# Third layer of a four-layer hybrid: the sums of squares of the heads' outputs as two products of operands in two parts

## The chip, the cores and the metric

The kernel runs on one core of one Trainium2 chip. The metric is the device time of one execution in microseconds (us), as the median of the runs taken. Five engines work beside each other, each through its own queue in order: TensorE (PE in the profile, its weight loads PEld), VectorE (DVE), ScalarE (ACT), GpSimd (POOL) and SyncE (SP), which here issues the DMAs.

## The reference

A stack of four residual layers over 1040 tokens (16 learned ones in front of 1024) of width 1024: a sliding-window attention, an mLSTM, an HGRN2 and again an attention. The change is in the third layer. Cut to what matters:

```python
def hgrn2_branch(u, w_in, lower_bound, o_gain, w_out, valid):
    q, fpre, inp, z = _split(u @ w_in, C_SIZES)
    ...
    o = hgrn2_chunkwise(heads(silu(q)), heads(kk), heads(inp), heads(lf))   # 8 heads of width 128
    o = rmsnorm(o, o_gain.reshape(C_HEADS, C_DV)).reshape(bsz, lp, C_W)     # over the 128 of each head
    return (o * silu(z)) @ w_out

def rmsnorm(x, g):
    return x * rsqrt(mean(x * x, axis=-1) + EPS) * g
```

For each head and token the mean of the squares of 128 numbers is needed. Everything is in fp32.

## The kernel before

**Layout.** Activations lie with their features on the 128 partitions and the tokens along the row: `x` as eight tiles of 128 x 1040. Tokens are worked on in three chunks, `CHUNKS`, of 400, 384 and 256 columns. A sum over features is thus a sum over partitions, and is made by a matmul with a 128 x 128 tile of ones (`rones`, type fp32r; `ones` is the same tile seen as fp32).

**Products in parts.** A large projection is made of operands in two parts: `split` (L186 to L188) writes a rounded high part (a cast to fp32r on ACT, L187) and the rest, source minus high part (a subtraction on DVE, L188). `proj` (L254), `proj_v` (L295, L299) and `proj_out` (L337) multiply these parts in three fp32r products. Other matmuls take fp32 operands as they are; the sums of squares of this layer are among them. The second layer's sums of squares (L1001) are already two products of a split operand with `rones`.

**One head of the third layer** (`mixer`, in `layer_c`). The tokens go through five regions `REGIONS`: the first block of 16, then four pairs of blocks of 128 (blocks 0; 1, 2; 3, 4; 5, 6; 7, 8). For each region:

- `level`: tiles `X` by additions on DVE (L1152, L1153, L1145), Exp on ACT (L1154, L1146) and a multiplication on DVE (L1155);
- `levels_mm`: a burst of small products of these on PE (L1168, L1178);
- `tail0`: the results are masked (DVE, L1195), summed (DVE, L1204) into `rd`, and GpSimd copies `rd` to the diagonal blocks of `att` (L1206, four copies);
- `tail1`: a transpose on PE (L1228), and its copy to SBUF, `kT` (ACT, L1230);
- `tail2`, block by block: `po` gets `V` times `att` (PE, L1243) and the state times the decayed queries (PE, L1245); then the state is renewed (PE L1250, DVE L1255), on which the next block's L1245 waits.

Three times in a head a chunk of `po` is complete: after block 3, 6 and 8. `o_evac` (L1259) then copies it to the head's row `R["o", h]` (ACT, L1261) and squares it into a temporary tile (ACT, L1263). Later `o_stat` (L1265) sums the squares over the partitions (PE, L1269), makes the reciprocal root from this (`rstd_from`: ACT Ln L353, Exp L354, in place in the tile that held the squares) and multiplies the row by gain and root (DVE, L1271). `o_stat(0)` comes after block 5, `o_stat(1)` after block 8, and `o_stat(2)` after block 0 of the next head; at the end of the last head it comes last. There are 8 heads and 24 such sums.

**What sets the order.** PE's order is written out: `body` weaves the steps of a head (with a cost in ns each, the first number of `S(...)`) with the projections of the next heads, in proportion to the costs (`weave`, L53). The other engines' instructions are put in order when the kernel is built, by a priority list; those under `hi` (all of `mixer`'s) go ahead of others by `PRIO`. Each engine then works its list strictly in order. Temporary tiles `t` share five slots (`TMPS`); PSUM tiles share eight.

Of the kernel before, what the change touches and what calls it, by code (L numbers as in the profile page):

```python
# [10 lines left out]
F32R = mybir.dt.float32r  # L11
# [4 lines left out]
P = 128  # L16
# [22 lines left out]
ROWS, TMPS, RAWS, YS, QS = 9, 5, 2, 3, 6  # L39
# [69 lines left out]
def hybrid_kernel(ctx: ExitStack, tc: tile.TileContext, ins, out, layers=(0, 1, 2, 3)):  # L109
    nc = tc.nc  # L110
    v, s, g, pe, sp = nc.vector, nc.scalar, nc.gpsimd, nc.tensor, nc.sync
# [5 lines left out]
    tpool = ctx.enter_context(tc.tile_pool(name="tpool", bufs=1))  # L117
# [5 lines left out]
    def nm(x):  # L123
        ctr[0] += 1
        return f"{x}{ctr[0]}"
# [10 lines left out]
    def tmp():  # L136
        return tpool.tile([P, 404], F32, tag="t", name=nm("t"), bufs=TMPS)
# [10 lines left out]
    def psa():  # L148
        return psum("pa", 1)
# [4 lines left out]
    rones = cpool.tile([P, P], F32R, name="ones")  # L154
    ones = rones.bitcast(F32)
# [30 lines left out]
    def split(src, h, l):  # L186
        s.copy(h, src)  # L187
        v.tensor_tensor(l, src, h.bitcast(F32), op=ALU.subtract)  # L188
# [163 lines left out]
    def rstd_from(acc, dst, cn, n):  # L352
        s.activation(dst[:, :cn], acc[:, :cn], AF.Ln, bias=eps, scale=1.0 / n)  # L353
        s.activation(dst[:, :cn], dst[:, :cn], AF.Exp, scale=-0.5)  # L354

    def hi(fn):
        def f():
            with tc.high_priority(offset=PRIO):
                fn()

        return f
# [687 lines left out]
    def layer_c(i, j, fin):  # L1049
        win, wout = ins["c_win"][j], ins["c_wout"][j]  # L1050
        R = {}
# [74 lines left out]
        REGIONS = ((0,), (1, 2), (3, 4), (5, 6), (7, 8))  # L1126

        def mixer(h):
            vs = slice((h % 2) * P, (h % 2) * P + P)
            W = {}  # L1130
# [101 lines left out]
            def tail2(r, b):  # L1232
                blkno = REGIONS[r][b]
                c0, cn = blk(blkno)
                n = [blkno in z for z in CHUNK_BLOCKS].index(True)
                if blkno == CHUNK_BLOCKS[n][0]:
                    if n == 0:
                        R["o", h] = row()
                    W["po"] = psum("po", 1)
                oc = slice(c0 - CHUNKS[n][0], c0 - CHUNKS[n][0] + cn)  # L1240
                V = R["v", h // 2, blkno]
                att = W["att", r] if r == 0 else W["att", r][:, b, :]
                pe.matmul(W["po"][:, oc], V[:cn, vs], att, start=True, stop=(r == 0))  # L1243
                if r:
                    pe.matmul(W["po"][:, oc], W["S"], W["qA", r][:, P * b : P * b + P], start=False, stop=True)  # L1245
                if blkno == CHUNK_BLOCKS[n][-1]:
                    o_evac(n)
                if blkno < NB - 1:
                    pc = psa()
                    pe.matmul(pc[:, :P], W["kT", r][:cn, P * b : P * b + P], V[:cn, vs], start=True, stop=True)  # L1250
                    Sn = R["mix"].tile([P, P], F32, tag="S", name=nm("S"), bufs=2)
                    if r == 0:
                        v.tensor_copy(Sn, pc[:, :P])
                    else:
                        v.scalar_tensor_tensor(Sn, W["S"], W["eL", r][:, b : b + 1], pc[:, :P],  # L1255
                                               op0=ALU.mult, op1=ALU.add)
                    W["S"] = Sn

            def o_evac(n):  # L1259
                c0, cn = CHUNKS[n]  # L1260
                s.copy(R["o", h][:, c0 : c0 + cn], W["po"][:, :cn])  # L1261
                W["sq", n] = sq = tmp()
                s.activation(sq[:, :cn], W["po"][:, :cn], AF.Square)  # L1263

            def o_stat(n):  # L1265
                c0, cn = CHUNKS[n]
                o, sq = R["o", h][:, c0 : c0 + cn], W["sq", n]
                st = psa()
                pe.matmul(st[:, :cn], ones, sq[:, :cn], start=True, stop=True)  # L1269
                rstd_from(st, sq, cn, 128)  # L1270
                v.scalar_tensor_tensor(o, o, R["ogain"][:, h : h + 1], sq[:, :cn], op0=ALU.mult, op1=ALU.mult)  # L1271

            def S(cost, fn, *a):
                return [cost, hi(lambda: fn(*a)), None]

            main, tails = [], []
            for r in range(5):
                lvs = list(range(8)) if r else [3, 4, 5, 6, 7]
                st = []
                for lv in lvs:  # L1280
                    st.append(S(0.0, level, r, lv))
                    st.append([GAP, lambda: None, None])
                st.append(S(BURST if r else 0.2 * BURST, levels_mm, r, lvs))
                st.append(S(0.0, tail0, r))
                main.append(st)
                ts = [S(214 if r else 107, tail1, r), [KT_LAG, lambda: None, None]]
                for b in range(len(REGIONS[r])):
                    ts.append(S(640, tail2, r, b))
                    if REGIONS[r][b] in (5, 8):
                        ts.append(S(666, o_stat, 0 if REGIONS[r][b] == 5 else 1))  # L1290
                tails.append(ts)
            return main, tails, S(427, o_stat, 2)

        fg = {h: f_proj(h) for h in range(8)}
        qg = {h: q_proj(h) for h in range(8)}
# [8 lines left out]
        for h in range(8):  # L1304
            fill = qg[0][2] if h == 0 else []
            if h in (4, 6):
                fill += flat(outs(oc[h - 3]))
            if h < 7:
                fill += flat(fg[h + 1]) + flat(qg[h + 1])
            if h in (1, 3, 5):  # L1310
                fill += flat(vg[h // 2 + 1])
            for z in {2: (0, 1), 4: (2,), 5: (3,), 7: (4, 5, 6)}.get(h, ()):
                fill += flat(zg[z])
            main, tails, end = mixer(h)
            if h:
                tails[0].append(held)
            held = end
            mx = []
            for r in range(5):
                mx += weave(main[r], last)  # L1320
                last = [[TAIL_LAG, lambda: None, None]] + tails[r]
            body += weave(mx, fill)
# [8 lines left out]
    for pos, i in enumerate(layers):  # L1331
# [30 lines left out]
        else:  # L1362
            h0, h1 = (sum(z[0] for z in head[k]) for k in range(2))
            seq = flat(head)
            for n, t0, t1, end in ((2, h0 + h1 * FIRST[2], h0 + h1 * FIRST[3], h0 + h1), (1, h0 * FIRST[0], h0 * FIRST[1], h0)):
                st = norm.stats(n, PARTS[n])
# [139 lines left out]
```

## Time and profile before

| | us |
|---|---|
| median of 3 runs | 2607.71 (2605.75 to 2611.24) |
| the profiled execution | 2610.83 |
| its span, first to last instruction | 2609.0 |
| PE busy, of the span | 2558.0 (98%) |
| DVE busy | 1980.3 (76%) |
| ACT busy | 1725.9 (66%) |
| POOL busy | 154.1 (6%) |
| granted TensorE clock, mean | 0.995 |

Busy is the time in which an engine had at least one instruction at work. PE's matmuls overlap each other, so their spacing (from one start to the next), not their recorded length, tells what they take from PE's time. Rows of the timeline give start and length in us, engine, line, operation, tiles written and read, and shape; in brackets the idle time before and what ended it. The third layer's mixers run from about 1590 to 2125 us of the span: the first small `level` tiles on DVE are at 1588.7, the last sum of squares on PE at 2122.1.

### The profile page before, as it was taken

The page shows a single profiled execution, that of the slowest core. Times are in us where ns is not written, and L with a number is a line of the kernel's source. Part 1 is how long each engine was busy: PE and PEld are TensorE (multiplying, and loading weights), DVE is VectorE, ACT ScalarE, POOL GpSimd, SP SyncE. Part 2 cuts the span into 40 slices and gives each one's busy share as a digit, 9 for nine tenths or more (in the row PEclk, how much of TensorE's full clock was granted, in tenths as well). Part 3 has the DMA queues.
Part 4 walks back from the last instruction along what each step waited for, and adds up shares of the span by engine and source line. Part 5 has one row for each costly group of instructions (what it writes and reads, how often), then busy time and mean ns, then how long its engine had stood idle before and what let it go on. Part 6 is the DMA issues. An engine that isn't in the chain of part 4 may idle for free.

```text
span 2609.0 us, 56062 instructions
## 1 busy us (share of the span) xinstructions
PE 2558.0 (98%) x21048; PEld 2459.0 (94%) x21048; DVE 1980.3 (76%) x5487; ACT 1725.9 (66%) x4757; POOL 154.1 (6%) x538
## 2 busy tenths in 40 slices
PE   7999999999999999999999999999999999999999
PEld 6899889899999999999999999999999999999999
DVE  6677777986767676767677788978787978677776
ACT  6777776566464646464646857878585867768872
POOL 1100100000000000000000000201001011000000
PEclk9999999999999999999999999999999999999999
DMA  4111111021111111111110101011110111111112
GB/s 136 56 43 50 46 37 47 17 67 58 41 58 41 58 41 58 41 58 41 55 61 34 57 27 42 30 38 34 34 42 26 42 62 45 54 44 47 53 38 82
DMA packets 74048, 126.81 MB, mean 49 GB/s; under 512 B 11552, under 2 KB 25760, under 8 KB 73776
## 3 DMA queue, kind: packets, MB, share of 16 engines
q1 hardware_dynamic: 73776, 123.23, 14.5%
q8 instruction: 165, 2.70, 0.4%
q14 instruction: 107, 0.88, 0.1%
HBM read 108.34 MB, written 4.26 MB: 43 GB/s over the span
## 4 chain that ended last, share of the span: by engine, by line
PE 81%; DVE 10%; ACT 6%; issue 1%; DMA 1%; POOL 0%; SPq 0%; DVEq 0%; ACTq 0%; POOLq 0%
PE pj L254 39%; PE pj L337 16%; PE pj L299 11%; PE po L682 2%; PE pt L660 1%; PE pm L614 1%; PE pm L615 1%; DVE t L407 1%; PE pa L534 1%; DVE ul L188 1%; PE po L918 1%; PE pj L295 1%; PE pm L890 1%; DVE X L1153 1%; DVE X L1155 1%
## 5 line engine op out<-in xcount | busy, mean ns | idle before, releaser
L254 PE MATMUL pj<-uh,wh 128*128 128x384 f32 (+2 forms) x2592 | 870.9, 336 | 3.7 <-ACT uh L187 3.6
L254 PE MATMUL pj<-ul,wh 128*128 128x384 f32 (+2 forms) x2592 | 835.3, 322 | 2.9 <-DVE ul L188 2.8
L254 PE MATMUL pj<-uh,wl 128*128 128x384 f32 (+2 forms) x2592 | 832.9, 321 | 0.1
L254 PEld LDWEIGHTS pj<-uh,wh 128*128 128x128 f32 x2592 | 491.3, 190 | 24.1 <-issue 12.7
L254 PEld LDWEIGHTS pj<-ul,wh 128*128 128x128 f32 x2592 | 491.2, 190 | 8.7 <-DVE ul L188 5.5
L254 PEld LDWEIGHTS pj<-uh,wl 128*128 128x128 f32 x2592 | 490.9, 189 | 0.5 <-DVE wl L188 0.4
L188 DVE TENSOR_TENSOR wl<-wr,wh 128x512 fp32r<-128x512 f32 x336 | 227.9, 687 | 58.1 <-ACT wh L187 55.4
L340 DVE TENSOR_TENSOR x<-x,pj 128x384 f32<-128x384 f32 (+2 forms) x480 | 235.4, 510 | 43.2 <-PE pj L337 41.3
L187 ACT CAST wh<-wr 128x512 fp32r<-128x512 f32 x337 | 203.3, 616 | 83.0 <-PE pj L337 26.8
L299 PE MATMUL pj<-wh,uh 128*128 128x256 f32 x896 | 258.1, 288 | 0.0
L337 PE MATMUL pj<-yh,wh 128*128 128x384 f32 (+2 forms) x768 | 253.0, 329 | 0.0
L299 PE MATMUL pj<-wh,ul 128*128 128x256 f32 x896 | 252.4, 282 | 0.0
L299 PE MATMUL pj<-wl,uh 128*128 128x256 f32 x896 | 252.3, 282 | 0.0
L337 PE MATMUL pj<-yl,wh 128*128 128x384 f32 (+2 forms) x768 | 247.4, 322 | 3.1 <-DVE yl L188 3.1
L337 PE MATMUL pj<-yh,wl 128*128 128x384 f32 (+2 forms) x768 | 246.8, 321 | 0.0
L299 PEld LDWEIGHTS pj<-wh,uh 128*128 128x128 f32 x896 | 169.3, 189 | 1.1 <-issue 0.3
L187 ACT CAST yh<-r 128x400 fp32r<-128x400 f32 (+2 forms) x144 | 68.6, 477 | 153.2 <-PE pj L337 141.7
L299 PEld LDWEIGHTS pj<-wl,uh 128*128 128x128 f32 x896 | 169.3, 189 | 0.5
L299 PEld LDWEIGHTS pj<-wh,ul 128*128 128x128 f32 x896 | 169.3, 189 | 0.0
L428 ACT ACTIVATE t<-t 128x384 f32<-128x384 f32 (+2 forms) x240 | 117.8, 491 | 76.5 <-DVE t L427 74.8
L427 DVE SCALAR_TENSOR_TENSOR t<-pj,t 128x384 f32<-128x384 f32 (+2 forms) x192 | 98.8, 514 | 78.2 <-ACT t L426 75.3
L337 PEld LDWEIGHTS pj<-yl,wh 128*128 128x128 f32 x768 | 144.9, 189 | 5.0 <-DVE yl L188 4.7
(265 smaller groups left out, 5431.4 us busy)
## 6 DMA issues: line engine op xcount, KB each, us to landing
wr<-in_b_win SPq DMA_DIRECT2D x128, 256.0 KB, 2.6
wr<-in_a_win SPq DMA_DIRECT2D x80, 256.0 KB, 2.7
wr<-in_c_win SPq DMA_DIRECT2D x64, 256.0 KB, 2.7
r<-rowsd SPq DMA_DIRECT2D x16, 520.0 KB, 5.4
wr<-in_a_wout SPq DMA_DIRECT2D x32, 256.0 KB, 2.7
wr<-in_b_wout SPq DMA_DIRECT2D x32, 256.0 KB, 2.6
t<-t SPq DMA_DIRECT2D x96, 48.0 KB, 1.9
wr<-in_c_wout SPq DMA_DIRECT2D x16, 256.0 KB, 2.7
```

The costliest lines, as they stand in the source:

```text
L187: s.copy(h, src)
L188: v.tensor_tensor(l, src, h.bitcast(F32), op=ALU.subtract)
L254: pe.matmul(acc[:, :cn], a[:, k, :], b[:, k, c0 : c0 + cn], start=(k == 0 and i == 0), stop=(k == KT - 1 and i == 2))
L295: pe.matmul(acc[:48, :256], um[:, k, :], m[:, kk, :], start=(k == 0 and m is wh), stop=(k == KT - 1 and m is wl))
L299: pe.matmul(acc[:cn, :256], a[:, k, c0 : c0 + cn], m[:, kk, :], start=(k == 0 and i == 0), stop=(k == KT - 1 and i == 2))
L337: pe.matmul(acc[:, :cn], a[:, k, mc], b, start=(k == 0 and i == 0), stop=(k == 1 and i == 2))
L340: v.tensor_tensor(x[:, m, c0 : c0 + cn], x[:, m, c0 : c0 + cn], acc[:, :cn], op=ALU.add)
L407: v.scalar_tensor_tensor(u, x[:, k, cs], ngain[:, self.i, k : k + 1], self.acc[n], op0=ALU.mult, op1=ALU.mult)
L427: v.scalar_tensor_tensor(a[:, :cn], z, 0.0, a[:, :cn], op0=ALU.min, op1=ALU.subtract)
L428: s.activation(a[:, :cn], a[:, :cn], AF.Exp)
L534: pe.matmul(st[:, 2 * k : 2 * k + 2], sq[:, z : z + P], R["masks"][:, 0:P:64], start=True, stop=True)
L682: pe.matmul(po[64 * hh : 64 * hh + 64, q0 - c0 : q0 - c0 + nq], V[kb][:kn, vc : vc + 64], ws[hh]["Pt"][:kn, u, ki, :nq], start=(ki == 0), ...
```

## The change

In `o_evac` the squares are now split at once: the high part goes into a tile `oh` (ACT cast, L187), of which there is one slot, and the rest into a tile `ol` (DVE subtraction, L188), which takes a slot of the `t` tiles until the sum is made. In `o_stat` the one fp32 product with `ones` becomes two fp32r products with `rones` that add up in the same PSUM tile, and a fresh temporary tile takes the root. The costs that the weave uses for the three steps are halved.

```diff
             def o_evac(n):
                 c0, cn = CHUNKS[n]
                 s.copy(R["o", h][:, c0 : c0 + cn], W["po"][:, :cn])
-                W["sq", n] = sq = tmp()
+                sq = tmp()
                 s.activation(sq[:, :cn], W["po"][:, :cn], AF.Square)
+                high = R["mix"].tile([P, 400], F32R, tag="oh", name=nm("oh"), bufs=1)
+                low = tpool.tile([P, 404], F32R, tag="t", name=nm("ol"), bufs=TMPS)
+                W["sq", n] = high, low
+                split(sq[:, :cn], high[:, :cn], low[:, :cn])
 
             def o_stat(n):
                 c0, cn = CHUNKS[n]
-                o, sq = R["o", h][:, c0 : c0 + cn], W["sq", n]
+                o, sq = R["o", h][:, c0 : c0 + cn], tmp()
                 st = psa()
-                pe.matmul(st[:, :cn], ones, sq[:, :cn], start=True, stop=True)
+                for z, part in enumerate(W.pop(("sq", n))):
+                    pe.matmul(st[:, :cn], rones, part[:, :cn], start=(z == 0), stop=(z == 1))
                 rstd_from(st, sq, cn, 128)
...
-                        ts.append(S(666, o_stat, 0 if REGIONS[r][b] == 5 else 1))
+                        ts.append(S(333, o_stat, 0 if REGIONS[r][b] == 5 else 1))
                 tails.append(ts)
-            return main, tails, S(427, o_stat, 2)
+            return main, tails, S(214, o_stat, 2)
```

Each engine's order differs from about the start of the third layer's mixers to their end and is the same again in the fourth layer. Three places, with the program's tile names and numbers (which differ between the two programs for the same tile).

DVE in the first head, where the last pair of blocks is prepared, before the change: the masking L1195 and the sum L1204 of the region with blocks 7 and 8.

```order
L1152 TENSOR_TENSOR X_21759<-r_20881,r_20882 128x64x2
L1271 SCALAR_TENSOR_TENSOR r_20868<-r_20868,ogain_20127,t_21283 128x400
L1195 TENSOR_TENSOR t_21512<-pm_21411,masks_20129 128x192 x2
L1255 SCALAR_TENSOR_TENSOR S_21510<-S_21477,s_21319,pa_21508 128x128
L1204 TENSOR_REDUCE rd_21515<-t_21512 128x64
```

The same place now (L1276 is the line that was L1271):

```order
L1152 TENSOR_TENSOR X_21775<-r_20874,r_20875 128x64x2
L1276 SCALAR_TENSOR_TENSOR r_20893<-r_20893,ogain_20127,t_21489 128x400
L1255 SCALAR_TENSOR_TENSOR S_21520<-S_21481,s_21323,pa_21518 128x128
L1153 TENSOR_TENSOR X_21765<-r_20874 128x16x8
L1153 TENSOR_TENSOR X_21775<-r_20874 128x64x2
L188 TENSOR_TENSOR ol_21515<-t_21512,oh_21514 128x384
L1195 TENSOR_TENSOR t_21522<-pm_21422,masks_20129 128x192 x2
L427 SCALAR_TENSOR_TENSOR t_21502<-pj_21406,t_21502 128x256
L1204 TENSOR_REDUCE rd_21525<-t_21522 128x64
```

The subtraction for the second chunk stands ahead of L1195, so L1195 and all behind it wait for the cast `oh` on ACT. In all eight heads `ol` of the 384 columns stands so, directly or one instruction ahead of this L1195.

ACT at the same place, before: the copy and the Square of the second chunk, among the steps of a projection's sigmoid (L424 to L426).

```order
L354 ACTIVATE t_21283<-t_21283 128x400
L1261 COPY r_20868<-po_21289 128x384
L424 ACTIVATE t_21496<-pj_21460 128x256
L1263 ACTIVATE t_21506<-po_21289 128x384
L425 ACTIVATE t_21496<-t_21496 128x256
L1154 ACTIVATE X_21744<-X_21744 128x256
```

ACT there now:

```order
L354 ACTIVATE t_21489<-t_21489 128x400
L1261 COPY r_20893<-po_21293 128x384
L424 ACTIVATE t_21502<-pj_21406 128x256
L1263 ACTIVATE t_21512<-po_21293 128x384
L425 ACTIVATE t_21502<-t_21502 128x256
L187 CAST oh_21514<-t_21512 128x384
L426 ACTIVATE t_21502<-t_21502,one 128x256
L1154 ACTIVATE X_21770<-X_21770 128x256
```

The cast stands one instruction behind the Square; in the second head an Exp (L354) stands between them.

ACT at the end of the last head, before: copy, Square, a sigmoid's steps, and the roots of the last two sums.

```order
L428 ACTIVATE t_29265<-t_29265 128x400
L1261 COPY r_28572<-po_29301 128x256
L1263 ACTIVATE t_29317<-po_29301 128x256
L424 ACTIVATE t_29325<-pj_29273 128x384
L425 ACTIVATE t_29325<-t_29325 128x384
L426 ACTIVATE t_29325<-t_29325,one 128x384
L353 ACTIVATE t_29203<-pa_29350,eps 128x384
```

And now:

```order
L424 ACTIVATE t_29456<-pj_29409 128x384
L1261 COPY r_28696<-po_29443 128x256
L1263 ACTIVATE t_29477<-po_29443 128x256
L425 ACTIVATE t_29456<-t_29456 128x384
L426 ACTIVATE t_29456<-t_29456,one 128x384
L428 ACTIVATE t_29456<-t_29456 128x384
L187 CAST oh_29479<-t_29477 128x256
L187 CAST wh_29920<-wr_29922 128x512
L353 ACTIVATE t_29502<-pa_29503,eps 128x384
```

The cast of the last chunk stands behind a whole sigmoid, with L428 in it, which waits for DVE's L427. On DVE, `ol` of the last chunk stands behind that sigmoid's L427 and L435. On PE there are now 18 matmuls of 256 columns from the last block's L1245 to the last head's `o_stat(1)`, 6 more to `o_stat(2)`, and behind that the output projection (L337); before, the two sums came after 6 matmuls of 384 and 6 of 256 columns, and after 12 more of 256.

## The prediction

> **What bounds the kernel now.** First the page's busy shares and the chain of work that ended last: is one engine the path, and where not?
>
> ```profile
> PE 2558.0 (98%) x21048; PEld 2459.0 (94%) x21048; DVE 1980.3 (76%) x5487; ACT 1725.9 (66%) x4757; POOL 154.1 (6%) x538
> PE 81%; DVE 10%; ACT 6%; issue 1%; DMA 1%; POOL 0%; SPq 0%; DVEq 0%; ACTq 0%; POOLq 0%
> ```
>
> PE is, but for a sixth of the span the chain runs through DVE and ACT. Next the same for the stretch of the change, in windows (length, then busy time of PE, PEld, DVE, ACT, POOL, the granted clock, DMA). I quote the first, the third, the last but one, and the sum of nine.
>
> ```profile
> 1590.00:1660.00 70.00, 65.38 (x843) 62.72 (x842) 60.70 (x210) 56.37 (x163) 6.56 (x14) 0.98 0.12 39
> ...
> 1720.00:1780.00 60.00, 59.60 (x797) 56.79 (x796) 53.97 (x182) 50.95 (x147) 6.28 (x16) 1.00 0.12 41
> ...
> 2020.00:2080.00 60.00, 58.16 (x792) 55.41 (x791) 55.30 (x187) 50.09 (x143) 6.29 (x16) 1.00 0.12 41
> ...
> sum 540.00, PE 529.81 PEld 507.79 DVE 453.80 ACT 404.47 POOL 56.91; mean PE 58.87 PEld 56.42 DVE 50.42 ACT 44.94 POOL 6.32
> ```
>
> PE idles 10.2 of 540 us, 6.5 of them in the first and the last window quoted, where DVE is at 87% and 92%; in the one between, DVE at 90% cost PE nothing. Over all nine DVE has 86 us to spare. Third, for whom PE waited there (total, times, longest):
>
> ```profile
> PE po L1245 <- DVE S L1255: 5.6, 12, 1.4
> PE pm L1178 <- DVE X L1155: 2.5, 1, 2.5
> ...
> PE po L1243 <- POOL att L1206: 0.6, 1, 0.6
> ```
>
> So the layer is bound by PE, and what it takes off PE counts in full as long as no wait takes its place.
>
> **What the products cost PE.** The 24 sums are 48 records. A 400-column sum, the next matmul but one and the one after it; then a 256-column sum in the same way; then the second layer's sum of 400 columns, which is already two fp32r products.
>
> ```profile
> L1269 PE MATMUL pa<-t,ones 128*128 128x400 f32 (+2 forms) x48 | 18.9, 476 | 0.2 <-ACT v L269 0.2
> ```
>
> ```profile
> 1653.59 0.83 PE L1269 MATMUL pa<-t,ones 128*128 128x400 f32 x2
> ...
> 1654.38 0.28 PE L254 MATMUL pj<-ul,wh 128*128 128x256 f32 x1
> 1654.50 0.28 PE L254 MATMUL pj<-uh,wl 128*128 128x256 f32 x1
> ```
>
> ```profile
> 1741.22 0.59 PE L1269 MATMUL pa<-t,ones 128*128 128x256 f32 x2
> ...
> 1741.83 0.34 PE L254 MATMUL pj<-ul,wh 128*128 128x384 f32 x1
> 1742.00 0.34 PE L254 MATMUL pj<-uh,wl 128*128 128x384 f32 x1
> ```
>
> ```profile
> 902.37 0.34 PE L1001 MATMUL pa<-yh,ones 128*128 128x400 f32 x1
> ...
> 902.74 0.35 PE L254 MATMUL pj<-uh,wh 128*128 128x400 f32 x1
> ```
>
> From 1653.59 to 1654.38 are 0.79 us, with one 256-column matmul in it, which takes 0.12 (1654.38 to 1654.50): the fp32 sum takes 0.67. The pair takes 902.74 - 902.37 = 0.37. Saved: 0.30. For 256 columns: 0.61 less one 384-column matmul of 0.17 is 0.44; the pair would be 2 x 0.12 = 0.24; saved 0.20. For 384 columns by the ratio of columns 0.29. A head saves 0.79, eight heads **6.3 us**.
>
> **What the split adds.** 24 casts and 24 subtractions, priced by those of the output projection, which have the same three shapes:
>
> ```profile
> L187 ACT CAST yh<-r 128x400 fp32r<-128x400 f32 (+2 forms) x144 | 68.6, 477 | 153.2 <-PE pj L337 141.7 <-DVE r L436 9.3 <-DVE x L340 1.1
> L188 DVE TENSOR_TENSOR yl<-r,yh 128x400 fp32r<-128x400 f32 (+2 forms) x144 | 74.0, 515 | 53.5 <-ACT yh L187 53.4
> ```
>
> ACT gets 24 x 0.477 = 11.4 us, DVE 24 x 0.515 = 12.4 us, half a microsecond in three of five regions of a head. DVE's 86 spare us hide that on average. What counts is who stands behind them. `oh` has one slot, so the third cast of a head waits for `o_stat(1)`; in the written order over a hundred matmuls lie between block 8 and `o_stat(2)`, and I cost that at nothing, except at the end of the last head, where it is 24. The steps that the order moves by some matmuls carry no work of their own, and no DMA of this layer changes its place.
>
> **A new wait for `att`.** The order puts `ol` of the second chunk ahead of the masking L1195, which must go through L1204 and four POOL copies before PE's L1243 of block 7. How much room is there? First head: ACT, DVE, POOL, PE.
>
> ```profile
> 1656.73 0.49 ACT L1263 ACTIVATE t<-po 128x384 f32<-128x384 f32 x1
> 1657.10 0.42 ACT L425 ACTIVATE t<-t 128x256 f32<-128x256 f32 x1
> 1657.41 0.42 ACT L1154 ACTIVATE X<-X 128x256 f32<-128x256 f32 x1
> ```
>
> ```profile
> 1656.78 0.62 DVE L1195 TENSOR_TENSOR t<-pm,masks 128x192 f32<-128x192 f32 x2
> 1657.31 0.34 DVE L1255 SCALAR_TENSOR_TENSOR S<-S,s,pa 128x128 f32<-128x128 f32 x1
> 1657.57 0.88 DVE L1204 TENSOR_REDUCE rd<-t 128x64 f32<-128x384 f32 x1
> ```
>
> ```profile
> 1658.57 2.64 POOL L1206 COPY att<-rd 32x64 f32<-32x64 f32 x4 [9.17 <-DVE rd L1204]
> ```
>
> ```profile
> 1661.28 0.47 PE L1243 MATMUL po<-att,v 128*128 128x128 f32 x2
> ```
>
> The copies ended at 1661.21, 0.07 before PE came. Now the chain begins at the Square: Square to the next ACT instruction 0.37, that one 0.31, the cast 0.48, `ol` 0.5, L1195 0.53, one more DVE instruction 0.26, L1204 0.88, to POOL 0.1: 3.4 us, with hops 3.5. With 2.64 for the copies it ends 6.1 us after the Square began, where PE wants it after 1661.28 - 1656.73 = 4.55: PE waits 1.6; with copies of 1.80 (the last head's, below) 0.75. I take 1.2. The second head:
>
> ```profile
> 1719.79 0.50 ACT L1263 ACTIVATE t<-po 128x384 f32<-128x384 f32 x1
> ```
>
> ```profile
> 1721.88 2.23 POOL L1206 COPY att<-rd 32x64 f32<-32x64 f32 x4 [15.04 <-DVE rd L1204]
> ```
>
> ```profile
> 1725.09 0.38 PE L1243 MATMUL po<-att,v 128*128 128x128 f32 x2
> ```
>
> Here the instruction between is an Exp of half a microsecond: 3.7 + 2.23 = 5.9 against 5.30, a wait of 0.6; with 1.80 for the copies 0.2. I take 0.4. In the other six the copies ended well ahead or, in one, already cost the 0.6 of the row above; the last head's:
>
> ```profile
> 2112.80 1.80 POOL L1206 COPY att<-rd 32x64 f32<-32x64 f32 x4 [10.84 <-DVE rd L1204]
> ```
>
> ```profile
> 2116.13 0.38 PE L1243 MATMUL po<-att,v 128*128 128x128 f32 x2
> ```
>
> 1.53 of room; I give the six 0.3 together. Sum **+1.9 us**, bounds 0.5 and 6 (below).
>
> **The end of the last head.** `oh` of the last chunk stands behind a whole sigmoid. The rows before:
>
> ```profile
> 2118.49 0.37 ACT L1261 COPY r<-po 128x256 f32<-128x256 f32 x1 [1.57 <-PE po L1245]
> 2118.76 0.39 ACT L1263 ACTIVATE t<-po 128x256 f32<-128x256 f32 x1
> ...
> 2120.07 0.52 ACT L425 ACTIVATE t<-t 128x384 f32<-128x384 f32 x1
> 2120.62 0.62 ACT L426 ACTIVATE t<-t,one 128x384 f32<-128x384 f32 x1
> ...
> 2122.17 0.51 ACT L428 ACTIVATE t<-t 128x384 f32<-128x384 f32 x1
> ```
>
> From the copy on: copy and Square 0.65, L425 0.5, L426 0.6, DVE's L427, about as long as a subtraction, 0.5, L428 0.5, then DVE's L435 0.5 beside the cast, `ol` 0.45: 3.7, with hops 4.1. PE needs it after 18 x 0.12 + 0.36 + 6 x 0.12 + 0.12 = 3.3. **+0.8**, bounds 0 (if the sigmoid starts earlier) and 1.5. Behind the sum stands an output projection that doesn't need it.
>
> **Sum.** -6.3 + 1.9 + 0.8 = -3.6 us. The profiled execution took 2610.83, its span 2609.0 and 1.8 around it: 2607.2. It lies 3.1 above the median of 2607.71, so against that **2604.1**; with the bounds of the waits (0.5 to 3.0, 0 to 1.5) 2601.9 to 2605.9. The irregular waits at the stretch's start (2.5 for L1155 above) may move either way under the new order; I take 0. A measurement of this kernel can tell about 0.2%, 5.2 us.
>
> **The rivals.**
>
> All hidden: in the new order the casts come soon enough everywhere. For it: the row with 1.53 of room, and only one wait of 0.6 for `att` in the whole layer now. Against it: 0.07 in the first head. 2607.71 - 6.3 = 2601.4, and 1 less if the start's waits shrink as well.
>
> `att` late in every head: POOL's copies get slow.
>
> ```profile
> L1206 POOL COPY att<-rd x128: 226/265/3692, 1626.5 to 2114.4; 32x64 f32<-32x64 f32 x128
> ```
>
> Four at the least would take 0.9 us, yet they took 2.64 in the first head; a copy (least, median and greatest in ns) can take 3.7. With 2.64 everywhere the first two heads wait 1.6 and 1.0; I put the six others between this and nothing, 0.6 each: 6 us. With the 0.8 of the end the gain is gone, -6.3 + 6.8: 2608.2. The Trainium skill, "SBUF — State Buffer", section "Who interferes with whom", has a mechanism for it: a DVE instruction with both inputs in SBUF and a GpSimd instruction that reads SBUF exclude each other, and `ol` has both in SBUF. By that rule 8 subtractions of 0.5 us could hold up the copies by 4 us in all, which would make of the forecast this rival's time. The spread in the row agrees with such a lock; but `ol` stands ahead of L1204, for which the copies wait, so it is over by then, and I add nothing for it.
>
> DVE becomes the path: if its 12.4 us find no cover, every burst L1178 and every L1245 comes later. -6.3 + 12.4 = +6.1: 2613.8, slower. For it: DVE at 92% in a window, and 2.5 + 5.6 us of PE's waits are for DVE. Against it: the window with DVE at 90% and PE at 99%, and 86 us to spare in the sum. It decides from where DVE has no gap left between one burst and the next.
>
> No gain on PE: the pair costs as much as the fp32 sum. The rows at 902 speak against it: 0 + 2.7, 2610.4.
>
> **How the numbers follow.** Forecast 0.52, all hidden 0.25, `att` late everywhere 0.15, DVE the path 0.06, no gain 0.02. Faster by over 0.2%: all hidden and the forecast's lower end, 0.25 + 0.05 = 0.30. Slower: 0.06. The rest, 0.64, within 0.2%. The range reaches from all hidden with a shorter start to `att` late everywhere with a measurement's spread: 2599.8 to 2609.8.
>
> **What would show it.** Right: the 24 sums as pairs, 0.37, 0.36 and 0.24 apart; PE waiting for POOL `att` at L1243 of block 7 in the first two heads, some 2 us in all; a short wait at the last L1274. Wrong: more than 4 us of waits for `att`, or PE's waits for DVE (8.1 us now) grown by over 2; or a gain of more than 6.3, which would have to come from the start of the stretch.

## The result, and the profile after

The changed kernel takes 2613.81 us (median of 22 runs, 2609.18 to 2616.40), the kernel before 2609.24 beside it (22 runs): a ratio of 1.0015, 95% interval 1.0010 to 1.0021. By this ratio it is 3.9 us slower (2.6 to 5.5), where 3.6 us faster was forecast; the two medians lie 4.6 us apart, and all differences below go by ratios. The profiled execution's span is 2612.5 us, 3.5 longer than before.

First the page of the changed kernel, its busy shares and its chain of work:

```profile
PE 2553.9 (98%) x21048; PEld 2456.8 (94%) x21048; DVE 1988.0 (76%) x5511; ACT 1729.0 (66%) x4781; POOL 143.7 (6%) x538
PE 78%; DVE 11%; ACT 7%; DMA 2%; issue 2%; POOL 0%; SPq 0%; DVEq 0%; ACTq 0%; POOLq 0%
```

PE is busy for 4.1 us less, yet the span is longer: PE waits more, and the chain runs more through DVE (11%, it was 10%) and ACT (7%, it was 6%). The same nine windows as before, their sum:

```profile
sum 540.00, PE 522.53 PEld 502.88 DVE 458.53 ACT 407.62 POOL 49.50; mean PE 58.06 PEld 55.88 DVE 50.95 ACT 45.29 POOL 5.50
```

PE idles 17.5 of 540 us now, 10.2 before. For whom it waits (total, times, longest):

```profile
PE po L1245 <- DVE S L1255: 11.6, 13, 2.0
PE po L1243 <- POOL att L1206: 2.5, 3, 1.3
PE pm L1178 <- DVE X L1155: 2.2, 1, 2.2
```

The waits for `att` grew by 1.9 us, the sum that was forecast. The 6.0 us more at L1245, for the renewed state `S`, were in no term of the forecast's sum. The largest of these waits is in head 3 (heads are counted from 0 from here on), between block 1 and block 2. PE before, then PE after, at that place; L1250 gives the product with which DVE renews `S`, the first L1245 behind it reads `S`:

```profile
1815.04 0.39 PE L1250 MATMUL pa<-v,kT 128*128 128x128 f32 x2
1815.18 0.37 PE L299 MATMUL pj<-wh,uh 128*128 128x256 f32 x1
...
1816.68 0.38 PE L1243 MATMUL po<-att,v 128*128 128x128 f32 x2
1817.39 0.49 PE L1245 MATMUL po<-X,S 128*128 128x128 f32 x2 [0.33 <-DVE S L1255]
```

```profile
1812.75 0.39 PE L1250 MATMUL pa<-v,kT 128*128 128x128 f32 x2
1812.98 0.39 PE L1243 MATMUL po<-att,v 128*128 128x128 f32 x2
1815.37 0.49 PE L1245 MATMUL po<-X,S 128*128 128x128 f32 x2 [2.00 <-DVE S L1255]
```

Before, twelve matmuls of a projection (L299) lay between L1250 and L1243; after, none. From L1250 to L1245 it takes 2.35 us before and 2.62 after: DVE's answer hardly changed, but PE has nothing to do meanwhile. What DVE does there now:

```profile
1812.67 0.81 DVE L1204 TENSOR_REDUCE rd<-t 128x64 f32<-128x384 f32 x1
1813.40 0.28 DVE L1152 TENSOR_TENSOR X<-r,r 128x128 f32<-128x128 f32 x1
...
1814.74 0.32 DVE L1155 TENSOR_TENSOR X<-X,Q 128x128 f32<-128x128 f32 x1
1814.98 0.33 DVE L1255 SCALAR_TENSOR_TENSOR S<-S,s,pa 128x128 f32<-128x128 f32 x1
```

DVE works without a gap, in its written order, on `rd`, on `X` tiles and on one tile `v` (L267, in the rows left out), which stand ahead of L1255. There is no `ol` among them.

### The profile page after: what moved, and what is told of

It is laid out like the page before. It is cut to its first block, busy times and chain, and to the rows that moved or that the text cites. A ratio compares the mean times of both kernels' runs of the same rounds, so it can differ in the third digit from the quotient of the medians.

```text
span 2612.5 us, 56091 instructions
## 1 busy us (share of the span) xinstructions
PE 2553.9 (98%) x21048; PEld 2456.8 (94%) x21048; DVE 1988.0 (76%) x5511; ACT 1729.0 (66%) x4781; POOL 143.7 (6%) x538
## 4 chain that ended last, share of the span: by engine, by line
PE 78%; DVE 11%; ACT 7%; DMA 2%; issue 2%; POOL 0%; SPq 0%; DVEq 0%; ACTq 0%; POOLq 0%
PE pj L254 37%; PE pj L337 16%; PE pj L299 11%; PE po L682 2%; PE pt L660 1%; PE pm L614 1%; DVE t L407 1%; PE pm L615 1%; PE pa L534 1%; DVE ul L188 1%; PE po L918 1%; PE pj L295 1%; DVE X L1152 1%; PE pm L890 1%; ACT Sm L639 1%
## 5 line engine op out<-in xcount | busy, mean ns | idle before, releaser
L188 DVE TENSOR_TENSOR wl<-wr,wh 128x512 fp32r<-128x512 f32 x336 | 227.3, 686 | 57.2 <-ACT wh L187 54.3
L187 ACT CAST wh<-wr 128x512 fp32r<-128x512 f32 x337 | 203.3, 617 | 84.1 <-PE pj L337 30.1
L299 PE MATMUL pj<-wh,uh 128*128 128x256 f32 x896 | 257.8, 288 | 0.0
L299 PE MATMUL pj<-wh,ul 128*128 128x256 f32 x896 | 252.7, 282 | 0.0
L299 PE MATMUL pj<-wl,uh 128*128 128x256 f32 x896 | 252.6, 282 | 0.0
L337 PE MATMUL pj<-yh,wh 128*128 128x384 f32 (+2 forms) x768 | 252.3, 329 | 0.0
L337 PE MATMUL pj<-yl,wh 128*128 128x384 f32 (+2 forms) x768 | 247.4, 322 | 3.1 <-DVE yl L188 3.1
L337 PE MATMUL pj<-yh,wl 128*128 128x384 f32 (+2 forms) x768 | 246.9, 321 | 0.0
L428 ACT ACTIVATE t<-t 128x384 f32<-128x384 f32 (+2 forms) x240 | 117.9, 491 | 80.7 <-DVE t L427 79.5
L299 PEld LDWEIGHTS pj<-wh,uh 128*128 128x128 f32 x896 | 169.4, 189 | 0.8 <-issue 0.3
L299 PEld LDWEIGHTS pj<-wl,uh 128*128 128x128 f32 x896 | 169.5, 189 | 0.2
L299 PEld LDWEIGHTS pj<-wh,ul 128*128 128x128 f32 x896 | 169.5, 189 | 0.0
L187 ACT CAST yh<-r 128x400 fp32r<-128x400 f32 (+2 forms) x144 | 68.6, 477 | 151.0 <-PE pj L337 139.5
L427 DVE SCALAR_TENSOR_TENSOR t<-pj,t 128x384 f32<-128x384 f32 (+2 forms) x192 | 98.4, 513 | 74.4 <-ACT t L426 73.2
L337 PEld LDWEIGHTS pj<-yl,wh 128*128 128x128 f32 x768 | 144.9, 189 | 4.7 <-DVE yl L188 4.7
```

The source lines that it names most:

```text
L299: pe.matmul(acc[:cn, :256], a[:, k, c0 : c0 + cn], m[:, kk, :], start=(k == 0 and i == 0), stop=(k == KT - 1 and i == 2))
L337: pe.matmul(acc[:, :cn], a[:, k, mc], b, start=(k == 0 and i == 0), stop=(k == 1 and i == 2))
L427: v.scalar_tensor_tensor(a[:, :cn], z, 0.0, a[:, :cn], op0=ALU.min, op1=ALU.subtract)
L428: s.activation(a[:, :cn], a[:, :cn], AF.Exp)
```

## The experiments

Each kernel ran beside the kernel before on the same chip (its median there was 2609.7 to 2611.6), and is given by its ratio to it. An interval is about 0.09% wide to each side, some 2.3 us, so a difference between two runs is known to some 3 us. The waits come from one profiled execution of each. Three theories were tested. A: the split's own work, on DVE above all, takes the gain back. B: a PE that is faster only comes earlier to the same waits. C: the halved cost numbers of the weave make an order of PE in which L1245 stands nearer behind L1250.

### e1: no split

```diff
-                sq = tmp()
-                s.activation(sq[:, :cn], W["po"][:, :cn], AF.Square)
-                high = R["mix"].tile([P, 400], F32R, tag="oh", name=nm("oh"), bufs=1)
                 low = tpool.tile([P, 404], F32R, tag="t", name=nm("ol"), bufs=TMPS)
-                W["sq", n] = high, low
-                split(sq[:, :cn], high[:, :cn], low[:, :cn])
+                s.activation(low[:, :cn], W["po"][:, :cn], AF.Square)
+                W["sq", n] = low, low
```

> No cast and no subtraction: the Square writes rounded squares into a tile of type fp32r, and both products read this one tile (the sum comes out doubled; left out is the correction by the low part). PE's order and work are those of the changed kernel. Theory A, the split's own work on DVE (12.4 us) and ACT (11.4 us) takes the gain back where DVE has no gap: without it PE waits at L1245 for S about 6 us, as in the kernel before, at L1243 for att under 1 us, and the time is 5 to 6 us under the kernel before. Theory B, DVE sets the pace in these places already and a faster PE only comes earlier to the same wait: the waits at L1245 stay at 10 us or more, and the time is within 1.5 us of the kernel before. Theory C, the new cost numbers of the weave make a worse order: as B, 0 to 2 us above the kernel before.

2607.78 us, ratio 0.9987 (0.9978 to 0.9996): 3.4 us under the kernel before, 7.3 under the changed one.

```profile
PE po L1245 <- DVE S L1255: 11.4, 13, 2.0
...
PE po L1243 <- POOL att L1206: 0.4, 1, 0.4
```

None of the three as written: A expected short waits at L1245, B a time within 1.5 us of the kernel before, C one of 0 to 2 us above it. Without the split the waits for `att` are back at what they were before the change; those at L1245 are all still there, so these are not the split's.

### e2: split made, fp32 sum

```diff
-                W["sq", n] = high, low
+                W["sq", n] = sq
...
-                for z, part in enumerate(W.pop(("sq", n))):
-                    pe.matmul(st[:, :cn], rones, part[:, :cn], start=(z == 0), stop=(z == 1))
+                pe.matmul(st[:, :cn], ones, W.pop(("sq", n))[:, :cn], start=True, stop=True)
```

> The split is made as in the changed kernel but not used; the sum is the one fp32 product of the unsplit squares, as in the kernel before. Theory A: the split's cost is additive, so the time is the changed kernel's plus most of the 6.3 us of PE: 8 to 10 us above the kernel before. Theory B: PE is slower, the waits at L1245 shrink from 11.6 to 6 or 7 us, and the time is about the changed kernel's, 3 to 5 us above the kernel before.

2617.37 us, ratio 1.0025 (1.0016 to 1.0033): 6.5 us above the kernel before, 2.6 above the changed one. That lies between what A and B expect, and the interval reaches both.

```profile
PE po L1245 <- DVE S L1255: 9.6, 13, 1.7
PE po L1243 <- POOL att L1206: 4.5, 5, 2.4
```

With the slow sums back on PE, the waits at L1245 are 9.6 us, not the 6 or 7 that B needs. With the split in place the two products thus save 2.6 us only, less than the 6.3 of the rows.

### e3: cast only

```diff
                 high = R["mix"].tile([P, 400], F32R, tag="oh", name=nm("oh"), bufs=1)
-                low = tpool.tile([P, 404], F32R, tag="t", name=nm("ol"), bufs=TMPS)
-                W["sq", n] = high, low
-                split(sq[:, :cn], high[:, :cn], low[:, :cn])
+                W["sq", n] = high, high
+                s.copy(high[:, :cn], sq[:, :cn])
```

> The cast to oh stays on ACT, the subtraction on DVE is gone; both products read oh (left out is the correction by the low part). Theory A with DVE as the place: 4 to 6 us under the kernel before, nearly as the run without any split. Theory A with ACT's casts as the place: 0 to 3 us above the kernel before. Theory B: within 1.5 us of the kernel before.

2608.10 us, ratio 0.9987 (0.9979 to 0.9996), 3.4 us under the kernel before, the same as without any split. The 24 casts on ACT cost nothing that shows. What the split costs in this order comes with the subtraction.

### e4: late subtraction

```diff
-                split(sq[:, :cn], high[:, :cn], low[:, :cn])
+                s.copy(high[:, :cn], sq[:, :cn])
+                W["lo", n] = lambda: v.tensor_tensor(low[:, :cn], sq[:, :cn], high[:, :cn].bitcast(F32), op=ALU.subtract)
+                if n == 2:
+                    W["lo", n]()
...
                     ts.append(S(640, tail2, r, b))
+                    if REGIONS[r][b] in (4, 7):
+                        ts.append(S(0, lambda n: W["lo", n](), 0 if REGIONS[r][b] == 4 else 1))
```

> The changed kernel, but the subtraction of the first two chunks of a head is issued a block later, so that it no longer stands ahead of the masking L1195 and the sum L1204. Theory A: the waits for att fall from 2.5 us to under 0.8, those at L1245 lose little, 9 to 11 us; 2 us under the changed kernel, 2 above the kernel before. Theory B: the same for att, and the waits at L1245 take it up again: within 1 us of the changed kernel. If the place of the subtraction ahead of L1204 is what delays DVE's list as a whole: 4 us or more under the changed kernel.

2610.86 us, ratio 0.9998 (0.9989 to 1.0007): 0.5 us under the kernel before and 4.4 under the changed one, as the third expectation had it.

```profile
PE po L1245 <- DVE S L1255: 11.2, 13, 2.0
...
PE pa L1277 <- DVE ol L1268: 1.2, 2, 0.9
PE po L1243 <- POOL att L1206: 0.5, 1, 0.5
```

In all heads the subtraction of the 384 columns now stands behind L1204, and the waits for `att` are 0.5 us, as before the change; two of the sums wait for `ol` instead (1.2). The waits at L1245 stay.

### e5: the kernel before with the new cost numbers

```diff
-                        ts.append(S(666, o_stat, 0 if REGIONS[r][b] == 5 else 1))
+                        ts.append(S(333, o_stat, 0 if REGIONS[r][b] == 5 else 1))
...
-            return main, tails, S(427, o_stat, 2)
+            return main, tails, S(214, o_stat, 2)
```

> The kernel before with the three cost numbers of the weave halved and nothing else: only the order changes. Theory B (a PE that is faster comes earlier to the same waits at L1245): waits at L1245 stay at 5 to 7 us and the time within 1.5 us of the kernel before. Theory C (the new costs, which pull the steps around them together, put L1245 nearer behind the renewal of S): waits at L1245 rise to 10 or 11 us, and the time is 3 to 5 us above the kernel before.

2613.82 us, ratio 1.0015 (1.0006 to 1.0024): 3.9 us slower with not one instruction added or made shorter. PE's waits, and the same place in head 3:

```profile
PE po L1245 <- DVE S L1255: 11.0, 13, 2.0
```

```profile
1816.69 0.39 PE L1250 MATMUL pa<-v,kT 128*128 128x128 f32 x2
1816.91 0.39 PE L1243 MATMUL po<-att,v 128*128 128x128 f32 x2
1819.29 0.49 PE L1245 MATMUL po<-X,S 128*128 128x128 f32 x2 [2.00 <-DVE S L1255]
```

The wait of 2.00 us of the changed kernel, with fp32 sums and no split. This is theory C; B falls. In PE's written order, the matmuls between the L1250 of block 1 and the next L1245 went from 13 to 1 in heads 1 and 3 and from 7 to 1 in head 7, in this kernel as in the changed one; the projection's group that stood there now stands behind L1245. At these three places the waits were 0.20 us, 0.33 and none in the kernel before; here they are 1.99, 2.00 and 1.03, which is 4.5 of the 5.4 us by which all waits at L1245 grew. In the changed kernel they are 1.36, 2.00 and 0.99, 3.8 of its 6.0.

### e6: the changed kernel with the old cost numbers

```diff
-                        ts.append(S(333, o_stat, 0 if REGIONS[r][b] == 5 else 1))
+                        ts.append(S(666, o_stat, 0 if REGIONS[r][b] == 5 else 1))
...
-            return main, tails, S(214, o_stat, 2)
+            return main, tails, S(427, o_stat, 2)
```

> The changed kernel with the old cost numbers 666, 666 and 427. Theory B: waits at L1245 near 11 us, the time within 1.5 us of the changed kernel, some 4 us above the kernel before. Theory C: waits at L1245 of 6 to 7 us, those for att stay near 2.5, and the time is 3 to 5 us under the changed kernel, that is within 1 us of the kernel before.

2609.73 us, ratio 0.9997 (0.9988 to 1.0006): 0.8 us under the kernel before, 4.7 under the changed one, as C expects. Its waits at L1245 are 8.9 us, more than the 6 to 7 expected; those for `att`, 3.0, are still there.

### e7: no split, old cost numbers

The edits of e1 and e6 together.

> Rounded squares in one tile for both products, without cast and subtraction, as in the first experiment, with the old cost numbers. Theory B: as that experiment, 3 to 4 us under the kernel before, waits at L1245 near 11 us. Theory C: the whole 6.3 us show, 6 to 7 us under the kernel before, waits at L1245 of 6 us.

2605.62 us, ratio 0.9981 (0.9972 to 0.9990): 5.0 us under the kernel before, with 6.6 us of waits at L1245. Nearer to C, though not the whole 6.3.

```profile
PE po L1243 <- POOL att L1206: 1.8, 2, 1.5
```

Waits for `att` are there with no split too: 1.5 us of these are in head 6, as they are in e14. So not all of the waits at this place in other kernels are the split's.

### e8: late subtraction, old cost numbers

The edits of e4 and e6 together.

> The late subtraction of the fourth experiment with the old cost numbers. Theory B: as that experiment, within 1.5 us of the kernel before. Theory C: 4 to 6 us under the kernel before, waits at L1245 of 6 us and for att under 0.8.

2606.90 us, ratio 0.9986 (0.9977 to 0.9995): 3.7 us under the kernel before, with the whole computation. No wait for `att` is left; those at L1245 are 8.9 us, where C expected 6 and e7, without the split, has 6.6. In this order the split seems to delay `S` as well.

### e9 and e10: the cost numbers by heads

e9 keeps the old numbers in heads 1, 3 and 7 alone, e10 in the five others alone:

```diff
-                        ts.append(S(333, o_stat, 0 if REGIONS[r][b] == 5 else 1))
+                        ts.append(S(666 if h in (1, 3, 7) else 333, o_stat, 0 if REGIONS[r][b] == 5 else 1))
...
-            return main, tails, S(214, o_stat, 2)
+            return main, tails, S(427 if h in (1, 3, 7) else 214, o_stat, 2)
```

(In e10 `h not in` for `h in`.) The weave of a head also holds the last sum of the head ahead of it, so the old numbers in one head do not by themselves bring its old order back.

> The changed kernel with the old cost numbers in heads 1, 3 and 7 only (counted from 0). In this order the matmuls between the product L1250 of block 1 and the next L1245 are, in these three heads, 1, 1 and 1, as in the changed kernel (13, 13 and 7 in the kernel before); the other heads mostly have the order of the old costs. Theory C1, these three places carry what the cost numbers do: as the changed kernel, 3 to 5 us above the kernel before, with waits of 1.1 to 2.2 us at each of the three. Theory C2, the cost numbers act through the order as a whole: as the changed kernel with all old costs, within 1.5 us of the kernel before.

2615.85 us, ratio 1.0021 (1.0012 to 1.0029), 5.5 us above the kernel before. The three waits are there (1.58, 1.31 and 0.78 by the rows of L1245, two of them within what C1 expected), so C1's side; but the run is no clean test, since this order has a wait that neither theory had:

```profile
PE po L1245 <- DVE S L1255: 9.9, 12, 1.9
PE pa L1250 <- ACT kT L1230: 4.5, 4, 1.7
```

> The other way round: the changed kernel with the old cost numbers in heads 0, 2, 4, 5 and 6 and the new ones in 1, 3 and 7. Here 13, 13 and 7 matmuls lie between L1250 of block 1 and L1245 in heads 1, 3 and 7, as in the kernel before, and as many at block 3 of these heads, where the kernel before has 1; but only 1 at block 1 of head 2. Theory C1: at most 1 us above the kernel before, the waits at L1245 under 9 us, none over 0.5 at the three places, and about 1 us at block 1 of head 2. Theory C2: 2 to 4 us above the kernel before.

2607.35 us, ratio 0.9988 (0.9979 to 0.9997): 3.1 us under the kernel before, 7.0 under the changed one, with the same instructions as the changed one. The place in head 3 once more, with its twelve matmuls back, and the total:

```profile
1814.93 0.39 PE L1250 MATMUL pa<-v,kT 128*128 128x128 f32 x2
1815.08 0.37 PE L299 MATMUL pj<-wh,uh 128*128 128x256 f32 x1
...
1816.58 0.38 PE L1243 MATMUL po<-att,v 128*128 128x128 f32 x2
1817.46 0.49 PE L1245 MATMUL po<-X,S 128*128 128x128 f32 x2 [0.50 <-DVE S L1255]
```

```profile
PE po L1245 <- DVE S L1255: 7.0, 10, 1.4
PE po L1243 <- POOL att L1206: 2.5, 3, 1.5
```

2.00 became 0.50 here, and the wait foretold for block 1 of head 2 is the longest (1.4). Head 1 kept 0.90, more than the 0.5 expected. The time is C1's. With the three places of e5 it says that the cost numbers act mostly by how many matmuls lie between L1250 and L1245; e9, which was to show the same from the other side, doesn't by itself.

### e11: late subtraction in the order of e10

The edits of e4 and e10 together.

> Both remedies: the late subtraction of the fourth experiment with the order of the run before this one. If the place of the subtraction and the three places at L1245 are all that took the gain: 4 to 5.5 us under the kernel before, waits for att under 0.8 us, at L1245 7 to 9. If something else is left: no better than 3 us under it.

2605.34 us, ratio 0.9975 (0.9965 to 0.9986): 6.5 us under the kernel before and 10.4 under the changed kernel, with the whole computation (7 runs). That is more than either expectation, though the interval reaches the first one's 4 to 5.5.

```profile
PE po L1245 <- DVE S L1255: 6.5, 9, 1.4
```

No wait for `att` stands in its list, and little is left for the sums (0.2 for `ol`).

### e12: one product of rounded squares

```diff
-                for z, part in enumerate(W.pop(("sq", n))):
-                    pe.matmul(st[:, :cn], rones, part[:, :cn], start=(z == 0), stop=(z == 1))
+                pe.matmul(st[:, :cn], rones, W.pop(("sq", n))[:, :cn], start=True, stop=True)
```

(with the Square of e1 and the old cost numbers)

> One product of the rounded squares alone (the Square writes fp32r; the correction by the low part is left out), with the old cost numbers: no split, and half of the changed kernel's sums on PE, which takes 3.9 us more off PE than two products. If PE's savings count in full where no work is added: 8 to 9 us under the kernel before. If a PE that comes earlier meets the waits at L1245 instead: 5 to 6 us under it, as with two products.

2603.84 us, ratio 0.9975 (0.9966 to 0.9983), 6.5 us under the kernel before and 1.5 under e7, between the two expectations; an interval of 2.3 us to each side doesn't tell 5.5 from 8.5. It gives up the low part and is no faster than e11, which keeps it.

### e13 and e14: the order of e10 by itself

e13 is the kernel before with the new numbers in heads 1, 3 and 7 alone; e14 is e1 with the numbers of e10.

> The kernel before, fp32 sums, with the new cost numbers in heads 1, 3 and 7 only, which gives PE the order of the two runs before the last. If that order is better by itself: 1 to 2.5 us under the kernel before, and the two products are worth 4 to 5 us of the 6.5 by which the late subtraction in this order was faster. If the order only undoes a harm that the faster sums bring: within 0.8 us of the kernel before, and all 6.5 belong to the products.

2611.06 us, ratio 1.0005 (0.9996 to 1.0014): 1.3 us above the kernel before, with 6.8 us of waits at L1245. The order by itself brings no gain that can be measured.

> Rounded squares in one tile for both products, without cast and subtraction, in the order of heads 1, 3 and 7. If PE's saving counts in full once the waits at L1245 are short: 6 to 8 us under the kernel before, and 5.5 to 6.5 under the kernel before in this order. If a faster PE still meets later S tiles: 4 to 5 us under the kernel before.

2604.18 us, ratio 0.9982 (0.9973 to 0.9991): 4.7 us under the kernel before and 6.0 under e13, by which PE's saving counts in full in this order. By itself 4.7 is nearer to the other expectation; the interval leaves both. So the 6.5 us of e11 are not the order's by itself.

### All together

Difference to the kernel before in us, from the ratios, each with some 2.3 to either side (e11 2.7, the change 1.4):

| | old cost numbers | new in all heads | new in heads 1, 3, 7 |
|---|---|---|---|
| fp32 sum, no split | 0 | +3.9 (e5) | +1.3 (e13) |
| two products, no split | -5.0 (e7) | -3.4 (e1) | -4.7 (e14) |
| two products, late subtraction | -3.7 (e8) | -0.5 (e4) | **-6.5 (e11)** |
| two products, as changed | -0.8 (e6) | **+3.9 (the change)** | -3.1 (e10) |
| fp32 sum, split made | | +6.5 (e2) | |

Down from the first row to the second: the products save 5.0, 7.3 and 6.0 us, 6.1 in the mean; with the split in place, from e2 to the change, 2.6. From the second row to the third: the split with a late subtraction costs 1.3, 2.9 and -1.8, 0.8 in the mean. From the third to the fourth: the early place costs 2.9, 4.4 and 3.4, 3.6 in the mean. From the first column to the second: the new numbers cost 3.9, 1.6, 3.2 and 4.7, 3.4 in the mean.

## Why the prediction was wrong, point by point

**The saving on PE, -6.3 us: right where there is no split.** The pairs are there, 0.36 from the `oh` product of 384 columns to the matmul behind the pair:

```profile
2124.15 0.34 PE L1274 MATMUL pa<-oh,ones 128*128 128x384 f32 x1
2124.33 0.34 PE L1274 MATMUL pa<-ol,ones 128*128 128x384 f32 x1
2124.51 0.28 PE L254 MATMUL pj<-uh,wh 128*128 128x256 f32 x1
```

The runs without the split measure 6.1 in the mean of three orders. With the split made for both (e2 against the change) it is 2.6, with some 2.7 to either side; why it is less there stays open. The rival that the pair costs as much as the fp32 sum is out.

**The split's work on DVE and ACT, at its price: right; hidden on average: right for ACT.** The groups of the changed kernel's stretch:

```profile
L188 DVE TENSOR_TENSOR ol<-t,oh 128x400 fp32r<-128x400 f32 (+2 forms) x24 | 12.4, 516 | 3.2 <-ACT oh L187 3.1
L187 ACT CAST oh<-t 128x400 fp32r<-128x400 f32 (+2 forms) x24 | 11.7, 486 | 0.4
```

12.4 us, as forecast, and 11.7 for 11.4. The casts cost nothing (e3 against e1). The subtractions cost little where they stand late (0.8 in the mean, not to be told from nothing) and 3.6 more where they stand early.

**The wait for `att`, +1.9 us: the places wrong, the sum right by luck, the price probably too low.** The waits grew by 1.9 us. But the first head has none: its four copies took 1.40 us, not the 2.64 of before, and ended just before PE came; the second has 0.5 (0.4 forecast). The rest is in heads 5 and 6, to which I gave next to nothing. Head 6, in the order ACT, DVE, POOL, PE:

```profile
2058.25 0.50 ACT L1263 ACTIVATE t<-po 128x384 f32<-128x384 f32 x1
2058.63 0.55 ACT L354 ACTIVATE t<-t 128x400 f32<-128x400 f32 x1
2059.06 0.52 ACT L187 CAST oh<-t 128x384 fp32r<-128x384 f32 x1
```

```profile
2059.21 0.64 DVE L1276 SCALAR_TENSOR_TENSOR r<-r,ogain,t 128x400 f32<-128x400 f32 x1 [0.46 <-ACT t L354]
2059.77 0.55 DVE L188 TENSOR_TENSOR ol<-t,oh 128x384 fp32r<-128x384 f32 x1
2060.24 0.61 DVE L1195 TENSOR_TENSOR t<-pm,masks 128x192 f32<-128x192 f32 x2
```

```profile
2061.97 1.94 POOL L1206 COPY att<-rd 32x64 f32<-32x64 f32 x4 [12.06 <-DVE rd L1204]
```

```profile
2063.97 0.38 PE L1243 MATMUL po<-att,v 128*128 128x128 f32 x1 [1.26 <-POOL att L1206]
```

This is the chain that was worked out for the first two heads, link by link: Square, one Exp between, cast, `ol`, L1195, L1204, copies; it ends at 2063.91, 5.7 us behind the Square's start. Yet the same L1243 of head 6 waits 0.57 us in the kernel before and 1.5 in e7 and e14, which have no split, so its 1.26 can't be put down to the split alone. The runs price the early place of the subtraction at 2.9 to 4.4 us, its waits at 2.0 to 3.0 (e4 against the changed kernel, e8 against e6, e11 against e10). The difference lies within their intervals and stays open.

**The end of the last head, +0.8 us: about right.** The last `oh` product starts 0.36 us behind the matmul ahead of it and the `ol` product 0.63 behind that, where 0.12 is the pace of 256 columns: 0.24 and 0.51 us late, 0.75 together. The cast stands where it was forecast, behind L428, at 2125.00.

**The order, 0 us: wrong, and what turned the sign.** The step that failed is this one: "The steps that the order moves by some matmuls carry no work of their own". They carry none, but they are what PE does while DVE renews `S`. The waits at L1245 grew by 6.0 us; e5 shows nearly the same growth (5.4), and 3.9 us, with the cost numbers alone. With the old numbers the changed kernel is not slower than the kernel before (e6, -0.8). I had listed the 5.6 us of these waits as the largest in the layer and counted the matmuls behind blocks for `o_stat`, but did not count them between L1250 and L1245, where the order shows 13 against 1.

**The rivals.** "DVE becomes the path" comes to the measured time, 2613.8, by another way: it let DVE's added work find no cover. The prediction named as a sign of being wrong that PE's waits for DVE grow by over 2 us. They did (8.1 to 13.8 for `S` and `X`), but with no split at all (e1) the waits at L1245 are as long, so that this rival met the time is luck. "All hidden" is out in the order of the change: the split costs 7.3 us there beside two products (e1 against the change) and 2.6 beside the fp32 sum (e5 against e2). "`att` late in every head" is out: three waits, and the copies got no slower (384 ns in the mean, 442 before).

**The range.** "All hidden" with a shorter start is 2600.4 by the prediction's own numbers, "`att` late in every head" 2608.2; the ends 2599.8 and 2609.8 add a spread whose size it doesn't derive.

**The sum as it should have been.** By the means of the table: -6.1 for the products, +4.4 for the split at its early place, +3.4 for the order, +1.7; measured +3.9. One change at a time gives +3.9 by construction, but splits it differently by the path. With the order first (e5, e2, the change): +3.9 for the order, +2.6 for the split, -2.6 for the products. With the order last (e7, e6, the change): -5.0 for the products, +4.2 for the split, +4.7 for the order. The forecast had -6.3, +2.7 and nothing. Both paths give the order some 4 us, which is more than enough for the wrong sign; how the products and the split share the rest is not resolved, with differences known to some 3 us.

## What to carry to other kernels

A cost number that a weave or planner uses is part of the program's order: when an edit changes it, count again what lies between each producer and its consumer on the engine that is bound, even if the new number is the true one. Here the halved numbers were about right for PE's time (333 and 214 ns for pairs of 360 to 370 and 240), and cost 3.4 us in the mean, mostly because they took the fill out from between L1250 and L1245; taken head by head and with the subtraction behind the step that others wait for, the same instructions are 10 us faster (e11). Split such a change on the chip into its order, its saving and its added work before the saving is doubted: here the products alone, without the split, were 3.4 to 5.0 us under the kernel before in every order.

## What the runs showed of the hardware

After the wait of 2.0 us in head 3 the changed kernel's matmuls of 256 columns went on at 0.12 us for some, then at 0.21, then at 0.12 again:

```profile
1815.37 0.49 PE L1245 MATMUL po<-X,S 128*128 128x128 f32 x2 [2.00 <-DVE S L1255]
...
1816.39 0.28 PE L299 MATMUL pj<-wl,uh 128*128 128x256 f32 x1
1816.51 0.36 PE L299 MATMUL pj<-wh,ul 128*128 128x256 f32 x1
1816.67 0.42 PE L299 MATMUL pj<-wh,uh 128*128 128x256 f32 x1
1816.88 0.42 PE L299 MATMUL pj<-wl,uh 128*128 128x256 f32 x1
...
1819.87 0.33 PE L299 MATMUL pj<-wh,uh 128*128 128x256 f32 x1
1820.04 0.28 PE L299 MATMUL pj<-wl,uh 128*128 128x256 f32 x1
```

From 1816.6 to 1819.9 they ran at little over half their pace, which cost some 1.6 us on top of the wait; the granted clock of this window is 0.97. The Trainium skill, "TensorE: Matmul & The Clock Gate", section "What's actually happening", has it that the clock is halved by a monitor with free-running windows of about 3.4 us, after a window that was idle. The length agrees (3.3 us). The idle time before does not: 2.4 us from the L1243 ahead of it to L1245, shorter than such a window, was enough here. In e5's profiled execution the same wait at the same place left the matmuls behind it at 0.12, so such a wait does not always bring the extra 1.6 us; that the windows run free would explain this, but no run here shows it.

These stretches don't account for the price of the order. The kernel before has one too: behind its wait of 2.46 us for `X` its matmuls of 400 columns lie 0.33 us apart from 1640.2 to 1642.6, against 0.18 just ahead of that, in the window whose granted clock is 0.98. And among the executions with a granted clock of 0.997, e5's three took 2612.6 us in the mean and the eight of the kernel before beside it 2609.2, a difference of 3.4.
